# k and v made token-major by VectorE block transposes and a trip through DRAM, in place of TensorE transposes, in a one-core hybrid trunk layer

## The chip, the cores and the metric

The kernel runs on one core of a Trainium2 chip. The metric is the device time of one execution in microseconds (us), as the median of several runs. In the profile the engines are PE (TensorE matmul), PEld (TensorE weight load), DVE (VectorE), ACT (ScalarE), POOL (GpSimd) and SP (SyncE, whose one queue issues every DMA of this kernel).

## The reference

One layer over 16 meta tokens and 2048 tokens of width 1024, all in float32. The part that the change touches is the gated DeltaNet group (8 heads of 128), chunk by chunk:

```python
q, k, v = jnp.split(jax.nn.silu(causal_dwconv(qkv, dn_conv_w)), 3, axis=-1)   # then per head, q and k normalised
kk = jnp.einsum('bhnid,bhnjd->bhnij', k, k)
a_low = jnp.where(strict, beta[..., :, None] * kk * decay, 0.0)
tmat = a_low + jnp.eye(CHUNK, dtype=a_low.dtype)
u = lax.linalg.triangular_solve(tmat, v * beta[..., None], left_side=True, lower=True, unit_diagonal=True)
w = lax.linalg.triangular_solve(tmat, k * (beta * jnp.exp(g))[..., None], left_side=True, lower=True, unit_diagonal=True)
...
def step(S, inp):
    u_c, w_c, qk_c, qd_c, kd_c, gl_c = inp
    v_new = u_c - jnp.einsum('bhcd,bhde->bhce', w_c, S)
    o = jnp.einsum('bhcd,bhde->bhce', qd_c, S) + jnp.einsum('bhij,bhje->bhie', qk_c, v_new)
    S = S * gl_c[..., None, None] + jnp.einsum('bhcd,bhce->bhde', kd_c, v_new)
    return S, o
```

Beside it stand a combined input projection (1024 to 8208 columns), a short gated convolution over another 1024 channels, the output projection (2048 to 1024), the residual and a final RMSNorm.

## The kernel before

The tokens are done in two halves (`hf` 0 and 1) of 1024, the first with the 16 meta tokens. **The main stream** is a list of jobs, 64 for each half: a job is one 128-column block of the input projection. It loads its weights (`load_w`, tile `wr`, two buffers), splits them in a high and a low part (`split_w`: `wh` on ACT, `wl` on DVE) and runs 24 matmuls for each token group (`run_group`, tile `mm`). So float32 accuracy is made of three passes: `hh`x`wh`, `hl`x`wh`, `hh`x`wl`. A job's result goes through a convolution on DVE (`acc`) to `k`, `q` or `vT`, or to a gate. These tiles are channel-major: channel on the partition, token along the row. After the jobs the output projection runs in units of 48 matmuls (`unit_mm`).

**The side streams** do the DeltaNet heads, one at a time: 16 pairs of half and head, `i` = 0 to 15. `delta_front` makes the 128x128 products of k and q for the 8 chunks of a head, sends the diagonal 32x32 blocks through DRAM (`nbd`, tile `nb`), inverts them row by row on DVE (`substitution`: `prod`, `XT`) and writes the result to DRAM (`xtd`). `delta_back` reads it back to `W`, and merges the 32-blocks to 64-blocks with small matmuls (the merges: `X`, `Q`, `p1` to `p4`). It also makes the token-major operands: `kd` from `k`, `vr` from `vT`, each in two groups of four 128x128 transposes on TensorE into PSUM (pool `pta`, tag `ta`, two buffers), evicted with a scale `cd` by ACT and a scale `ir` by DVE. `delta_scan` runs the 8 chunks of the recurrence (PE `rec` and `o`, DVE `yy` and `S`, ACT `vn`), and reads `kd` and `vr`. `delta_out` normalises and gates. In the first half `normalize` also prepares rows of the second half's tokens, in the tile `kd`.

**What sets the order.** On PE, DVE, ACT and POOL the instructions run in the order in which they are written. A planner in the program sets that order: it keeps a clock of its own for each engine, and after every few matmuls of the main stream `pump()` lets each side stream that its clock calls ready write its next piece. The order of the DMAs on SP is set by the framework's scheduler. A DMA there also waits on one of eight semaphores, which it takes over from the DMA eight issues ahead. `hold(tag)` keeps two streams from one tile. Every instruction is recorded through one helper, so the profile puts nearly all of them on line L118, and tiles tell them apart.

Of the kernel before, what the change touches and what calls it, by code (L numbers as in the profile page):

```python
# [19 lines left out]
NM = 16  # L20
# [153 lines left out]
def hybrid_trunk(  # L174
# [24 lines left out]
    ged = tc.dram_tile([2, NH * 9, 128], F32, name="ged")  # L199
    nmd = tc.dram_tile([2, NM, NM], F32, name="nmd")  # L200
# [317 lines left out]
    def normalize(i):  # L518

        xt = vt(dp, [128, NC, 128], "kd").rearrange("p c i -> p (c i)")  # L520
        nc.sync.dma_start(xt, xs[HALF + 128 * i :][:128])
        yield after(xt)
        st = statistics(xt, 128, vt(dp, [128, 1840], "gw", dt=BF16))
        gains = []
        yield from hold("Q", True)

        def gain(c2):
            gains.append(vt(dp, [128, NC, 64], "Q").rearrange("p c i -> p (c i)"))
            nc.sync.dma_start(gains[c2], norm_g[0, 512 * c2 : 512 * c2 + 512].partition_broadcast(128))

        gain(0)
        yield after(gains[0], st[1])
        rs = refine(st, 128)
        for c2 in range(2):
            xc = xt[:, 512 * c2 : 512 * c2 + 512]
            nc.vector.scalar_tensor_tensor(xc, xc, rs, gains[c2], op0=ALU.mult, op1=ALU.mult)
            if c2 == 0:
                gain(1)
                yield after(gains[1])
        held.discard("Q")  # L540
        nc.sync.dma_start(xnd[i], xt)
        done.add(("xn", i))
# [34 lines left out]

    G = {}

    def gates(hf):  # L580
# [20 lines left out]
        pt = ptile(pta, "ta", [128, 512])  # L601
        gw = vt(dp, [128, 920], "gw")
# [82 lines left out]
        nc.sync.dma_start(ged[hf, :Wd], gT[:Wd])  # L685
        G[hf] = dict(beta=beta, gcum=gcum, neg=neg, nch=nch)
# [422 lines left out]

    def delta_back():  # L1110

        for i in range(2 * NH):
# [19 lines left out]
            while ("conv", hf, 16 + hd, LAST[hf]) not in done:  # L1132
                yield 0.3
            for b4 in range(2):
                cs = slice(4 * b4, 4 * b4 + 4)
                yield after(slot=(pta, "ta"), least=0.3)
                yield from hold()
                pk = ptile(pta, "ta", [128, 4, 128])
                for c in range(4):
                    tr(pk[:, c, :], k_[:, 4 * b4 + c, :])  # L1140
                for c in range(4):
                    cc = 4 * b4 + c
                    nc.scalar.activation(kd[:, cc], pk[:, c, :], AF.Copy, scale=cd[:, cc : cc + 1])
                yield after(d["vT"], slot=(pta, "ta"), least=0.3)
                yield from hold()
                pv = ptile(pta, "ta", [128, 4, 128])
                for c in range(4):
                    c0 = m0 + 128 * (4 * b4 + c)
                    tr(pv[:, c, :], d["vT"][:, c0 : c0 + 128])
                nc.vector.tensor_tensor(  # L1150
                    out=vr[:, cs],
                    in0=pv,
                    in1=ir[:, cs].unsqueeze(2).to_broadcast([128, 4, 128]),
                    op=ALU.mult,
                )
# [8 lines left out]
            done.add(("vr", i))  # L1164
# [18 lines left out]
            for a in (0, 64):  # L1183
                nc.scalar.activation(Q[a + 32 : a + 64, :, 0:32], p1[a + 32 : a + 64, :, 0:32], AF.Copy)
            nc.vector.tensor_copy(egl, qd[:, :, 127])
# [24 lines left out]
            for c in range(NC):  # L1210
                mmf(p4[0:64, c, :], lhsT=Q[64:128, c, :], rhs=W[64:128, c, 64:128])
            held.discard("Q")
            done.add(("merged", i))
            nc.scalar.mul(W[0:64, :, 64:128], p4[0:64], -1.0)
            yield after(W, qd)
# [164 lines left out]

    STEP = 1.0
# [110 lines left out]
    start(delta_front())  # L1492
    start(delta_back())
# [143 lines left out]
```

## Time and profile before

| | before |
|---|---|
| time, median of 3 runs (lowest to highest) | 2236.77 us (2235.26 to 2238.23) |
| the profiled execution's own time | 2236.26 us |
| its span from first to last instruction | 2234.5 us |
| busy share: PE, DVE, ACT, POOL | 97%, 65%, 38%, 8% |
| DMA: share of 16 engines, MB moved | 46.0%, 197.14 MB |
| mean granted TensorE clock | 0.992 of full speed |

The profiled execution stands 0.5 us under the median. Of its time 1.8 us lie outside the span. Matmuls are pipelined, so the durations of matmuls overlap, and their cost is read from the distance between starts.

### The profile page before, as it was taken

To read this page: it belongs to the slowest core of one execution; us is meant where nothing else is said; L and a number is where in the kernel's file an instruction comes from. 1 tells how busy PE (TensorE), PEld (TensorE's weight loads), DVE (VectorE), ACT (ScalarE), POOL (GpSimd) and SP (SyncE) were. 2 spreads that over 40 slices of the span, in tenths; PEclk is the share of its full clock that TensorE was granted. 3 is DMA by queue.
4 is the path that set the end of the run, shared out by engine and by line. 5 is a ranking of instruction groups with operands and counts; after the bars stand their busy time and mean duration, and the time that the engine had idled before them with its cause. 6 is when DMAs were issued, how large, how long until landed. Compare 5 with 4: busy or idle time off the path is not lost.

```text
span 2234.5 us, 35464 instructions
## 1 busy us (share of the span) xinstructions
PE 2174.5 (97%) x13472; PEld 1917.1 (86%) x13472; DVE 1451.7 (65%) x3919; ACT 854.0 (38%) x1987; POOL 189.3 (8%) x345
## 2 busy tenths in 40 slices
PE   6999999999998999999999999999999999999998
PEld 6999999999998999977888888888888877888886
DVE  4677777677775668686767677676767674444422
ACT  5533434343443334444344352425252523332211
POOL 4010101010101010111010101010101000000000
PEclk9999999999999999999999999999999999999999
DMA  5434544353446744523444423343677343645521
GB/s 140 76 77 67 86 70 95 64 95 65 92 61 78 83 76 89 131 43 60 82 70 65 83 57 78 53 78 53 79 52 75 60 114 126 203 170 188 188 91 57
DMA packets 258537, 199.41 MB, mean 89 GB/s; under 512 B 62117, under 2 KB 226478, under 8 KB 258366
## 3 DMA queue, kind: packets, MB, share of 16 engines
q1 hardware_dynamic: 258366, 197.14, 46.0%
q8 instruction: 106, 1.74, 0.3%
q14 instruction: 65, 0.53, 0.1%
HBM read 160.51 MB, written 36.59 MB: 88 GB/s over the span
## 4 chain that ended last, share of the span: by engine, by line
PE 88%; DMA 4%; DVE 3%; ACT 2%; SPq 1%; issue 1%; POOL 0%; POOLq 0%; ACTq 0%; DVEq 0%
PE mm L118 75%; PE ta L118 7%; PE rec L118 4%; PE o L118 2%; DMA kd<-in_x_dram 2%; SPq L118 1%; ACT junk L118 1%; DMA wr<-in_w_in_dram 1%; DMA nb<-nbd 1%; DVE prod L118 1%; DMA xtd<-XT 0%; DVE wl L118 0%; DVE XT L118 0%; ACT wh L118 0%; DVE acc L118 0%
## 5 line engine op out<-in xcount | busy, mean ns | idle before, releaser
L118 PE MATMUL mm<-hh,wh 128*128 128x512 f32 (+3 forms) x2816 | 1008.4, 366 | 8.7 <-ACT hh L118 6.7
L118 PE MATMUL mm<-hl,wh 128*128 128x512 f32 (+3 forms) x2816 | 985.4, 357 | 0.4 <-DVE hl L118 0.4
L118 PE MATMUL mm<-hh,wl 128*128 128x512 f32 (+3 forms) x2816 | 640.1, 360 | 1.7 <-DVE wl L118 1.7
L118 PEld LDWEIGHTS mm<-hh,wh 128*128 128x128 f32 x2816 | 533.1, 190 | 60.3 <-ACT hh L118 7.9
L118 PEld LDWEIGHTS mm<-hl,wh 128*128 128x128 f32 x2816 | 532.5, 190 | 48.1 <-DVE hl L118 1.9
L118 PEld LDWEIGHTS mm<-hh,wl 128*128 128x128 f32 x2816 | 479.6, 189 | 48.9 <-DVE wl L118 2.2
L118 DVE TENSOR_TENSOR wl<-wr,wh 128x512 fp32r<-128x512 f32 x356 | 238.3, 689 | 97.6 <-ACT wh L118 77.0
L118 DVE SCALAR_TENSOR_TENSOR acc<-raw,pcol,acc 128x384 f32<-128x384 f32 (+2 forms) x360 | 232.9, 649 | 87.9 <-ACT acc L118 83.8
L118 ACT ACTIVATE wh<-wr 128x1024 fp32r<-128x1024 f32 x182 | 191.9, 1055 | 88.7 <-PE mm L118 49.7
L118 DVE SCALAR_TENSOR_TENSOR prod<-nb,XT 128x8 f32<-128x8 f32 (+30 forms) x496 | 191.0, 385 | 22.7 <-DMA nb<-nbd 19.1
L118 DVE TENSOR_REDUCE XT<-prod 128x8 f32<-128x16 f32 (+30 forms) x496 | 147.2, 297 | 17.0
L118 ACT ACTIVATE vn<-rec,cj 128x128 f32<-128x128 f32 x128 | 46.9, 366 | 248.4 <-PE rec L118 248.1
L118 ACT ACTIVATE raw<-mm 128x384 f32<-128x384 f32 (+2 forms) x120 | 61.5, 513 | 192.7 <-PE mm L118 192.2
L118 PE MATMUL mm<-oh,wh 128*128 128x512 f32 x256 | 101.9, 398 | 0.0
L118 ACT ACTIVATE sc_c<-mm 128x384 f32<-128x384 f32 (+3 forms) x82 | 42.1, 515 | 154.4 <-PE mm L118 154.3
L118 PE MATMUL mm<-ol,wh 128*128 128x512 f32 x256 | 100.4, 392 | 0.0
L118 DVE SCALAR_TENSOR_TENSOR yy<-rec,neg,vr 128x128 f32<-128x128 f32 x128 | 44.5, 348 | 56.1 <-PE rec L118 55.5
L118 DVE TENSOR_TENSOR y<-mm,y 128x512 f32<-128x512 f32 x21 | 14.5, 691 | 101.1 <-PE mm L118 101.1
L118 ACT ACTIVATE ojk<-y 128x512 bf16<-128x512 f32 x21 | 13.2, 631 | 164.6 <-DVE y L118 127.1
L118 DVE SCALAR_TENSOR_TENSOR S<-S,egl,rec 128x128 f32<-128x128 f32 x104 | 35.7, 343 | 59.6 <-PE rec L118 59.1
L118 POOL TENSOR_TENSOR opy<-mo,nhalf 128x4 f32<-128x4 f32 x32 | 34.3, 1073 | 460.3 <-DVE mo L118 451.5
L118 POOL TENSOR_SCALAR_AFFINE_SELECT E<-E 128x1024 f32<-128x1024 f32 x16 | 18.3, 1143 | 641.8 <-PE ta L118 352.3
(240 smaller groups left out, 2574.4 us busy)
## 6 DMA issues: line engine op xcount, KB each, us to landing
wr<-in_w_in_dram SPq DMA_DIRECT2D x128, 512.0 KB, 7.8
wr<-mixd SPq DMA_DIRECT2D x54, 512.0 KB, 4.3
E<-gtd SPq DMA_DIRECT2D x16, 512.0 KB, 3.8
qd<-ged SPq DMA_DIRECT2D x16, 512.0 KB, 6.4
nb<-nbd SPq DMA_DIRECT2D x64, 128.0 KB, 2.8
mixd<-zs SPq DMA_DIRECT2D x32, 256.0 KB, 2.4
out_dram<-y SPq DMA_DIRECT2D x16, 512.0 KB, 2.7
kd<-in_x_dram SPq DMA_DIRECT2D x9, 512.0 KB, 7.6
```

What stands on the lines that cost most here:

```text
L118: r = real(*args, **kw)
```

## The change

For each head a new side stream, `delta_turn`, takes `k` as soon as its convolution is done, and `vT` as soon as its own is, in two halves of four chunks each. `turn_out` transposes the 32x32 blocks of a 128x512 half on DVE into a temporary tile (the tags `gw` and `Q`, which exist already), and four DMAs write it to a new DRAM buffer `kvd`, so that the blocks land in transposed places: each moves 32 partitions in pieces of 32 floats (128 bytes). `delta_back` then reads `kd` and `vr` back from `kvd` by one DMA each, in pieces of 128 floats. The scale `cd` is now multiplied into the whole `kd` by POOL, and `ir` into the whole `vr` by DVE. The 16 TensorE transposes of k and v and their 10 evictions per head are gone; the 8 transposes of q stay. The job of the next `vT` now waits for the copy of `vT` to be issued, not for `delta_back`.

```diff
+    kvd = tc.dram_tile([2, 2, NC, 128, 128], F32, name="kvd")
...
+    def turn_out(dram, src, tmp):
+        nc.vector.transpose(out=tmp.rearrange("p c i -> p (c i)"), in_=src.rearrange("p c i -> p (c i)"))
+        for a in range(4):
+            nc.sync.dma_start(
+                dram[:, :, 32 * a : 32 * a + 32].rearrange("c (b y) x -> y (c b) x", b=4),
+                tmp[32 * a : 32 * a + 32].rearrange("y c (b x) -> y (c b) x", b=4),
+            )
...
+    def delta_turn():
+        for i in range(2 * NH):
+            hf, hd = divmod(i, NH)
+            m0 = NM if hf == 0 else 0
+            while i >= 2 and ("blocks", i - 2) not in done:
+                yield 0.3
+            for w in range(2):
+                while ("conv", hf, (8, 16)[w] + hd, LAST[hf]) not in done:
+                    yield 0.3
+                src = slot[i]["k"] if w == 0 else slot[i]["vT"][:, m0 : m0 + HALF].rearrange("p (c i) -> p c i", i=128)
+                for c2, tag in enumerate(("gw", "Q")):
+                    yield after(src, slot=(dp, tag), eng="DVE", lag=0.3)
+                    yield from hold(tag, True)
+                    cs = slice(4 * c2, 4 * c2 + 4)
+                    turn_out(kvd[i % 2, w, cs], src[:, cs], vt(dp, [128, 4, 128], tag))
+                    if w and c2:
+                        done.add(("vr", i))
+                    yield DRAIN
+                    held.discard(tag)
+            done.add(("turned", i))
...
-            while ("conv", hf, 16 + hd, LAST[hf]) not in done:
+            while ("turned", i) not in done:
                 yield 0.3
+            for w, t_ in enumerate((kd, vr)):
+                nc.sync.dma_start(t_, kvd[i % 2, w].rearrange("c t j -> t c j"))
             for b4 in range(2):
-                cs = slice(4 * b4, 4 * b4 + 4)
-                yield after(slot=(pta, "ta"), least=0.3)
-                yield from hold()
-                pk = ptile(pta, "ta", [128, 4, 128])
-                for c in range(4):
-                    tr(pk[:, c, :], k_[:, 4 * b4 + c, :])
-                for c in range(4):
-                    cc = 4 * b4 + c
-                    nc.scalar.activation(kd[:, cc], pk[:, c, :], AF.Copy, scale=cd[:, cc : cc + 1])
-                yield after(d["vT"], slot=(pta, "ta"), least=0.3)
-                yield from hold()
-                pv = ptile(pta, "ta", [128, 4, 128])
-                for c in range(4):
-                    c0 = m0 + 128 * (4 * b4 + c)
-                    tr(pv[:, c, :], d["vT"][:, c0 : c0 + 128])
-                nc.vector.tensor_tensor(
-                    out=vr[:, cs],
-                    in0=pv,
-                    in1=ir[:, cs].unsqueeze(2).to_broadcast([128, 4, 128]),
-                    op=ALU.mult,
-                )
...
+            nc.gpsimd.tensor_tensor(
+                out=kd, in0=kd, in1=cd.unsqueeze(2).to_broadcast([128, NC, 128]), op=ALU.mult
+            )
             nc.vector.tensor_copy(egl, qd[:, :, 127])
...
+            nc.vector.tensor_tensor(
+                out=vr, in0=vr, in1=ir.unsqueeze(2).to_broadcast([128, NC, 128]), op=ALU.mult
+            )
             held.discard("Q")
             done.add(("merged", i))
             nc.scalar.mul(W[0:64, :, 64:128], p4[0:64], -1.0)
-            yield after(W, qd)
+            yield after(W, qd, kd, vr)
...
+    start(delta_turn())
     start(delta_back())
```

**PE, pair i = 11 (second half, head 3), just ahead of its merges.** `x4` counts equal instructions in a row, and `ta<-ident,k` is a transpose of k. Before:

```order
L118 MATMUL ta<-ident,k 128x128 x4
L118 MATMUL mm<-hl,wh 128x512
L118 MATMUL mm<-hh,wh 128x512
L118 MATMUL ta<-ident,vT 128x128 x4
L118 MATMUL mm<-hl,wh 128x512
L118 MATMUL mm<-hh,wl 128x512 x2
L118 MATMUL ta<-ident,q 128x128 x4
L118 MATMUL mm<-hh,wl 128x512 x6
```

After:

```order
L118 MATMUL mm<-hh,wl 128x512 x3
L118 MATMUL ta<-ident,q 128x128 x4
L118 MATMUL mm<-hh,wl 128x512 x2
L118 MATMUL ta<-ident,q 128x128 x4
L118 MATMUL mm<-hh,wl 128x512 x3
```

The groups of k and v are gone from among the matmuls of the main stream, and nothing takes their place on PE.

**SP, pair i = 12 (second half, head 4), around the read of `W`.** `xtd<-XT` writes the inverted blocks and `W<-xtd` reads them back. Before:

```order
L118 DMA wr<-in_w_in_dram 128x8x128 x3
L118 DMA xtd<-XT 32x8x32 x4
L118 DMA W<-xtd 32x8x32 x4
L118 DMA E<-gtd 128x1024
```

After:

```order
L118 DMA kd<-kvd 128x8x128
L118 DMA mixd<-sc_y 128x4x128
L118 DMA qd<-ged 128x1024
L118 DMA mixd<-sc_y 128x4x128
L118 DMA wr<-in_w_in_dram 128x8x128
L118 DMA mixd<-zs 128x4x128
L118 DMA wr<-in_w_in_dram 128x8x128
L118 DMA kvd<-gw 32x16x32 x4
L118 DMA kvd<-Q 32x16x32 x4
L118 DMA wr<-in_w_in_dram 128x8x128
L118 DMA xtd<-XT 32x8x32 x4
L118 DMA vr<-kvd 128x8x128
```

The next row is again `W<-xtd`. Eight writes of v and the read of `vr` now stand just ahead of it, and the read of `kd` some way earlier. Such a read stands between `xtd<-XT` and `W<-xtd` in 3 of the 16 pairs (5, 12 and 13).

**POOL, pair i = 11, around its new multiplication.** `E<-E` belongs to the front of the next head, and `kpy` too. After:

```order
L118 COPY raw<-qcar 128x3 x2
L118 AFFINE_SELECT E<-E 128x1024
L118 TENSOR_TENSOR kd<-kd,cd 128x1024
L118 COPY sc_u<-ucar 128x2
L118 TENSOR_TENSOR kpy<-ssk,nhalf 128x8
```

Before, `COPY sc_u` followed `AFFINE_SELECT E<-E` directly.

## Rows read from the trace of the kernel before

**Rows 1.** The page, part 1: busy us, share of the span and instructions.

```profile
PE 2174.5 (97%) x13472; PEld 1917.1 (86%) x13472; DVE 1451.7 (65%) x3919; ACT 854.0 (38%) x1987; POOL 189.3 (8%) x345
```

**Rows 2.** Stretches of 50 us: busy us (instructions), clock, DMA share, GB/s.

```profile
700.00:750.00 50.00, 46.21 (x278) 45.90 (x277) 30.31 (x114) 17.96 (x44) 3.12 (x7) 0.94 0.72 90
...
1500.00:1550.00 50.00, 50.00 (x332) 40.52 (x331) 36.43 (x69) 26.24 (x57) 1.81 (x3) 1.00 0.36 52
...
1850.00:1900.00 50.00, 46.16 (x300) 36.30 (x299) 21.15 (x41) 17.50 (x37) 1.01 (x1) 0.90 0.33 108
```

**Rows 3.** PE in order of time, pair 11: start us, us, what.

```profile
1412.32 0.60 PE L118 MATMUL ta<-ident,k 128*128 128x128 f32 x4
1412.67 0.48 PE L118 MATMUL mm<-hh,wh 128*128 128x512 f32 x1
1412.99 0.39 PE L118 MATMUL mm<-hl,wh 128*128 128x512 f32 x1
1413.22 0.60 PE L118 MATMUL ta<-ident,vT 128*128 128x128 f32 x4
```

**Rows 4.** Groups by shape, of what goes: busy us, mean ns | idle before.

```profile
L118 ACT ACTIVATE kd<-ta,cd 128x128 f32<-128x128 f32 x128 | 36.3, 369 | 17.2 <-PE ta L118 15.8 <-DMA W<-xtd 1.4
...
L118 DVE TENSOR_TENSOR vr<-ta,ir 128x512 f32<-128x512 f32 x32 | 21.9, 685 | 6.8 <-PE ta L118 6.6
...
L118 PE MATMUL ta<-ident,vT 128*128 128x128 f32 x128 | 20.5, 283 | 1.2 <-ACT junk L118 0.7
...
L118 PE MATMUL ta<-ident,k 128*128 128x128 f32 x128 | 19.7, 277 | 1.3 <-ACT junk L118 1.3
```

**Rows 5.** What PE waited for: us, times, longest.

```profile
PE ta L118 <- DVE vr L118: 2.3, 1, 2.3
```

**Rows 6.** Groups by shape nearest to the new VectorE work.

```profile
L118 DVE TENSOR_TENSOR wl<-wr,wh 128x512 fp32r<-128x512 f32 x356 | 238.3, 689 | 97.6 <-ACT wh L118 77.0 <-PE mm L118 20.2
...
L118 DVE STREAM_TRANSPOSE X<-W 32x256 f32<-32x256 f32 x48 | 20.7, 432 | 2.2 <-DMA W<-xtd 1.1
...
L118 DVE TENSOR_TENSOR E<-E,cj 128x1024 f32<-128x1024 f32 x16 | 19.9, 1245 | 0.0
```

**Rows 7.** The tile kd: ns min/median/max, first and last start us.

```profile
L118 ACT ACTIVATE kd<-ta,cd x128: 342/368/395, 198.7 to 1846.0; 128x128 f32<-128x128 f32 x128
```

**Rows 8.** All engines, from 949 us: a POOL operation beside VectorE.

```profile
949.20 0.14 DVE L118 SCALAR_TENSOR_TENSOR msm<-mnb,mXT 16x4 f32<-16x4 f32 x1
...
949.59 2.70 POOL L118 TENSOR_TENSOR wl<-wr,wh 128x1024 fp32r<-128x1024 f32 x1 [16.39 <-ACT wh L118]
...
950.27 2.04 DVE L118 SCALAR_TENSOR_TENSOR msm<-mnb,mXT 16x5 f32<-16x5 f32 x1
```

**Rows 9.** The DMA queue, then issues: KB each, median us to landing.

```profile
q1 hardware_dynamic: 258366, 197.14, 46.0%
...
wr<-in_w_in_dram SPq DMA_DIRECT2D x128, 512.0 KB, 7.8
wr<-mixd SPq DMA_DIRECT2D x54, 512.0 KB, 4.3
...
nbd<-E SPq DMA_DIRECT2D x64, 32.0 KB, 1.9
xtd<-XT SPq DMA_DIRECT2D x64, 32.0 KB, 4.2
W<-xtd SPq DMA_DIRECT2D x64, 32.0 KB, 1.9
```

**Rows 10.** SP in order of time: the reads of W of pair 11.

```profile
1418.38 1.78 SPq L118 DMA_DIRECT2D W<-xtd  x4
```

**Rows 11.** VectorE in order of time: the transposes of W, pair 11.

```profile
1424.46 0.75 DVE L118 SCALAR_TENSOR_TENSOR acc<-raw,pcol,acc 128x512 f32<-128x512 f32 x1 [6.46 <-ACT acc L118]
1425.12 1.36 DVE L118 STREAM_TRANSPOSE X<-W 32x256 f32<-32x256 f32 x3
```

**Rows 12.** The same of pair 13.

```profile
1641.41 0.43 DVE L118 STREAM_TRANSPOSE X<-W 32x256 f32<-32x256 f32 x1 [0.64 <-DMA W<-xtd]
```

More of the change, by code (lines that the diff above doesn't have):

```diff
@@ L522, in normalize @@
         yield after(xt)
+        yield from hold("gw")
         st = statistics(xt, 128, vt(dp, [128, 1840], "gw", dt=BF16))
@@ L601, in gates @@
         pt = ptile(pta, "ta", [128, 512])
+        yield from hold("gw", True)
         gw = vt(dp, [128, 920], "gw")
@@ L685, in gates @@
         nc.sync.dma_start(ged[hf, :Wd], gT[:Wd])
+        held.discard("gw")
         G[hf] = dict(beta=beta, gcum=gcum, neg=neg, nch=nch)
@@ L1163, in delta_back @@
                     nc.scalar.activation(junk[:, 0:128], pq[:, c, :], AF.Square, accum_out=ssq[:, cc : cc + 1])
-            done.add(("vr", i))
             egl = vt(dp, [128, NC], "egl")
@@ L1379, in delta_out @@
             yield 0.3
+    DRAIN = 4.0
     STEP = 1.0
```

## The prediction, made before the changed kernel was run

> **What bounds the kernel now.** First the page's busy shares [rows 1]: PE is busy 97% of the span, DVE 65%, ACT 38%, POOL 8%. A busy PE need not be a full one, so the stretches come next [rows 2]. From 1500 to 1550 us PE has no idle time at the full granted clock while DVE is busy 36.4 of 50 us: here PE runs through its written order and nothing else limits it. At 700 to 750 and at 1850 to 1900 us PE stands idle for 3.8 us each and the granted clock drops to 0.94 and 0.90; in the first of these the DMA share is 0.72, twice the 0.36 of the clean stretch. So for most of the span the time is the sum of what PE is given, and in a few stretches it is a wait in the side streams. A change that takes work off PE should therefore show nearly in full, as long as it opens no new wait there. PE takes its order as written, so any wait of a side stream that the planner's clocks did not foresee stops the main stream too.
>
> **The change part by part.**
>
> *Transposes off PE.* How much a group of four costs is read from starts, not durations, which overlap. The k group starts at 1412.32 us, the v group at 1413.22, and between them stand the k group and two matmuls [rows 3]. The second of these takes 0.23 us to the next start, so the group takes 0.90 - 2 x 0.23 = 0.44 us. There are 128 + 128 such transposes [rows 4], 64 groups: 64 x 0.44 = 28.2 us off PE. The order shows that the matmuls around them simply close up. In the clean stretches this is on the path.
>
> *Waits that stood at them.* PE waited once for the eviction of `vr`, 2.3 us [rows 5]; that goes. The idle time just before the k and v groups is 1.3 + 1.2 us in all [rows 4], put down mostly to ACT's evictions of q, which stay. I take 2.3 us, with 0 and 4.8 us as bounds.
>
> *Evictions off ACT and DVE.* 128 ACT copies of 369 ns and 32 DVE multiplications of 685 ns go [rows 4]. ACT is at 38% and off the path: I cost that at nothing.
>
> *Work onto DVE.* 64 block transposes of 128x512. The nearest rows are the same operation at 32x256, 432 ns, and another operation at 128x512, 689 ns [rows 6]. The bounds are the second and twice the first, 0.69 to 0.86 us; I take 0.70, 64 x 0.70 = 44.8 us. The 16 multiplications of `vr` at 128x1024 cost 1.245 us each as the like one [rows 6], 19.9 us, against 21.9 us that go. DVE gains 43 us, and goes from 65% to about 67%. The 13.6 us that it has free in a clean stretch of 50 [rows 2] hide this, at 2.7 us per head. A head comes round every (1846.0 - 198.7) / 15 = 110 us, by the first and the last eviction of k [rows 7]. Without that cover it would cost up to 43 us.
>
> *Work onto POOL.* 16 multiplications of `kd` at 128x1024. POOL's own multiplication of that size took 2.70 us [rows 8], so about 43 us on an engine at 8%. Its price lies elsewhere. While it ran, a tiny DVE operation with two SBUF inputs (`msm`) that had taken 0.14 us took 2.04 us [rows 8]: DVE lost 1.9 us. Everything behind it on DVE waits too: `acc`, `wl`, the scan's `yy`, and PE for those. The bounds are 0 and 16 x 1.9 = 30.4 us. POOL's new operation stands behind the select of the next head's `E`, about where DVE in pair 11 sat idle for 6.46 us just before the transposes of `W` [rows 11]. So I take a sixth, 0.3 us per head, 5 us.
>
> The Trainium skill (SBUF — State Buffer, SBUF: two separate sides) calls this an exclusive lock, held for the whole instruction, by whichever of a GpSimd operation and a DVE operation with two SBUF inputs starts first. The trace agrees so far: 2.04 us for 0.14. By the page DVE would lose up to the whole 2.70 us each time, and the sum at its worst would be 43.2 instead of 30.4 us.
>
> *DMA.* Per head 16 writes of 64 KB in 128-byte pieces and two reads of 512 KB in 512-byte pieces: 8192 + 2048 packets and 2.1 MB. Before, the queue moved 197.14 MB in 258366 packets at 46.0% of the engines' span [rows 9], 1028 us of all sixteen. By bytes a head's share is 2.1/197.14 x 1028 = 11 us, by packets 10240/258366 x 1028 = 41 us, of 110 us per head. The nearest row, `nbd<-E`, 32 KB in 256 such pieces, lands in 1.9 us [rows 9], which lies near the lower end. I take 13 us: the share goes from 46% to near 58%. A weight load lands in 7.8 us [rows 9] and is issued about a job and a half ahead, so it has room. What has little room is the read of `W`, which PE's merges wait for. In pair 11 its four issues end at 1420.2 us [rows 10]; 1.9 us of landing [rows 9] counted from the last, which is issued some 0.45 us earlier, gives 1421.6, and DVE takes `W` up at 1425.1 [rows 11]: 3.5 us of room. Pair 13 has none: DVE there waits for the DMA itself [rows 12]. Queued on SP behind the new writes, which wait for DVE's transposes, are weight loads, `xtd` and `W`; `kd` and `vr` themselves are needed only by the scan, behind the merges. I add 4 us, one more stall like that of 700 to 750 us [rows 2], for the stretches in which the queue is already full. The bounds are 0 and rival C's.
>
> The Trainium skill (DMA: Bandwidth & Descriptors, Specifications) says that pieces under 512 bytes fall short of line rate, since the engine reads, modifies and writes. No row here sets such pieces beside long ones at equal load; if the rule bites, the share goes towards the 41 us end, and the wait is that of rival C.
>
> *Sum.* Against the profiled execution's own 2236.3 us, 0.5 us under the median: 2236.3 - 28.2 - 2.3 + 5 + 4 = 2214.8, so 2215 us.
>
> **The rivals.**
>
> *A. Nothing is given back.* DVE's free time hides both the transposes and POOL's hold, and `W` lands in its room everywhere. For it: the clean stretches, and that PE hardly ever waits for DVE there [rows 2]. Against it: the full queue at 700 us. 2236.3 - 28.2 - 2.3 = 2205.8 us.
>
> *B. POOL's hold on DVE reaches PE in full.* For it: the 1.9 us that DVE lost [rows 8], which the planner's clocks do not know of. Against it: the idle DVE at that place [rows 11]. 2205.8 + 30.4 = 2236.2 us: no change. The page on SBUF would make it 2205.8 + 43.2 = 2249 us, if every hold lasted the whole operation and reached PE.
>
> *C. `W` comes late, and it ends slower.* One queue serves all. The two reads of 1 MB per head and the writes of v get between `xtd<-XT` and the landing of `W`, the merges of each head wait, and PE with them. In the order such a read stands exactly there in 3 pairs, and writes of v just ahead of it in most. Each 512 KB in 512-byte pieces lands in 4.3 to 7.8 us [rows 9], so 2.4 to 5.9 us over a small one. If `W` is late by d, a head loses d - 3.5 us: 2205.8 + 5 + 16 x (d - 3.5). It decides from d = 5.1 us on, where the gain is gone. One slow read ahead of it, d = 5.9, gives 2249 us. Against it: `xtd` itself takes 4.2 us to land [rows 9], and `W` waits for that anyway, so a read issued between the two runs beside that wait.
>
> **How the numbers follow.** My forecast, 2205 to 2226 us around 2215, gets 0.60, A 0.13, B 0.12, C 0.15. What a measurement of this kernel can tell from no change is about 0.2%, 4.5 us, so faster is under 2232.3 and slower over 2241.2. Faster: the forecast, A, and a little of B, 0.74. Same: most of B and the mild end of C, 0.12. Slower: the rest of C, 0.14. The range starts at the lower bound, 2236.3 - 28.2 - 4.8 = 2203, and reaches to 2241 over B and the mild end of C, which leaves out about 0.14.
>
> **What would show it.** Right: 256 fewer PE transposes and no `kd<-ta` on ACT; in a clean stretch PE again without idle time; about 28 us fewer between the first and last matmul there; DVE near 67% busy; block transposes near 0.70 us; `kvd` writes landing in about 2 to 4 us. The hold shows as a DVE operation with two SBUF inputs that lasts 2 us beside POOL's `kd`, with or without a PE wait on DVE behind it. Rival C shows as DVE waiting for `W<-xtd` ahead of `X` in many pairs, and PE `ta` waiting on `X`. I would be wrong if PE's idle time grows by more than about 15 us, at whatever place, or if the block transposes take well over 0.86 us, so that DVE runs behind everywhere.

## The result and the profile after

The changed kernel takes 2265.95 us (median of 4 runs, 2261.55 to 2272.59), the kernel before 2236.33 us beside it: ratio 1.0134, 95% interval 1.0107 to 1.0161. It is 30 us slower (1.3%), where 22 us faster was forecast. The profiled execution is the longest of the four, 2272.59 us with a span of 2271.0 us; the mean granted clock is 0.978, before 0.992.

The page's busy shares of the changed kernel, to be held against [rows 1]:

```profile
PE 2168.2 (95%) x13216; PEld 1911.9 (84%) x13216; DVE 1485.6 (65%) x3963; ACT 818.5 (36%) x1857; POOL 220.1 (10%) x361
```

The 256 transposes are gone from PE, yet its busy time fell by 6.3 us only, and its idle time grew from 60.0 to 102.8 us (span less busy time). The prediction had named more than 15 us of added idle time as a sign of being wrong. Stretches of the changed kernel: length, busy us of PE, PEld, DVE, ACT and POOL, then clock, DMA share and GB/s. The first three answer to [rows 2].

```profile
700.00:750.00 50.00, 47.03 (x284) 46.51 (x283) 31.13 (x113) 17.11 (x43) 2.81 (x5) 0.93 0.88 93
...
1500.00:1550.00 50.00, 50.00 (x234) 41.17 (x233) 39.31 (x97) 16.98 (x39) 2.73 (x4) 1.00 0.68 110
...
1850.00:1900.00 50.00, 41.36 (x174) 32.23 (x173) 38.65 (x89) 18.78 (x42) 3.16 (x2) 0.92 0.52 161
```

```profile
1100.00:1600.00 500.00, 495.72 (x2905) 411.28 (x2904) 372.14 (x928) 190.46 (x428) 50.54 (x67) 1.00 0.54 88
550.00:1000.00 450.00, 418.59 (x2907) 402.47 (x2906) 314.32 (x961) 165.96 (x417) 53.02 (x81) 0.95 0.64 98
1600.00:1950.00 350.00, 324.32 (x1792) 265.13 (x1791) 220.93 (x533) 121.53 (x271) 25.13 (x32) 0.95 0.65 99
```

The same three wide stretches of the kernel before:

```profile
1100.00:1600.00 500.00, 499.81 (x2975) 415.06 (x2975) 356.79 (x903) 199.02 (x470) 41.27 (x63) 1.00 0.41 68
550.00:1000.00 450.00, 432.62 (x3020) 409.93 (x3019) 320.97 (x987) 180.66 (x454) 44.62 (x78) 0.98 0.52 81
1600.00:1950.00 350.00, 341.92 (x1925) 280.13 (x1924) 221.20 (x517) 135.80 (x311) 20.25 (x27) 0.98 0.56 101
```

The middle stretch is nearly as clean as it was: PE idles 4.3 us in it, before 0.2. Most of the loss lies in the other two, where the second half's rows are prepared and where the jobs end; they are called the full stretches below. There PE idles 14.0 + 17.6 = 31.6 us more, and the clock of what it does run is lower: 418.59 x 0.05 + 324.32 x 0.05 = 37.1 us below full speed against (432.62 + 341.92) x 0.02 = 15.5, so some 22 us more. That is an estimate from clocks rounded to 0.01, but it agrees with the 28.2 us that the prediction counted off PE, of which its busy time shows 6.3. By this estimate an idle us cost nearly two here.

What PE waits for in the changed kernel (us in total, times, longest):

```profile
PE ta L118 <- DVE X L118: 21.3, 10, 9.6
PE mm L118 <- ACT hh L118: 13.2, 3, 7.1
PE ta L118 <- issue: 10.6, 4, 7.5
PE mm L118 <- DVE sc_y L118: 6.9, 1, 6.9
```

The wait on `vr` [rows 5] is gone; waits on `X`, the transposed `W`, lead instead. The DMA queue and its issues (KB each, median us to landing), beside [rows 9]:

```profile
q1 hardware_dynamic: 426094, 229.14, 55.5%
...
wr<-in_w_in_dram SPq DMA_DIRECT2D x128, 512.0 KB, 9.0
...
kvd<-gw SPq DMA_DIRECT2D x128, 64.0 KB, 5.3
kvd<-Q SPq DMA_DIRECT2D x128, 64.0 KB, 2.5
...
vr<-kvd SPq DMA_DIRECT2D x16, 512.0 KB, 7.7
kd<-kvd SPq DMA_DIRECT2D x16, 512.0 KB, 4.2
...
xtd<-XT SPq DMA_DIRECT2D x64, 32.0 KB, 4.8
W<-xtd SPq DMA_DIRECT2D x64, 32.0 KB, 2.0
```

How `W` comes late is seen in pair 13, first on SP, then on DVE:

```profile
1636.62 8.49 SPq L118 DMA_DIRECT2D kvd<-gw  x4
1645.21 4.16 SPq L118 DMA_DIRECT2D kvd<-Q  x4
1649.48 0.44 SPq L118 DMA_DIRECT2D wr<-in_w_in_dram  x1
1650.02 5.67 SPq L118 DMA_DIRECT2D xtd<-XT  x4
1655.80 0.39 SPq L118 DMA_DIRECT2D vr<-kvd  x1
1665.79 1.78 SPq L118 DMA_DIRECT2D W<-xtd  x4
```

```profile
1647.41 0.42 DVE L118 TENSOR_REDUCE XT<-prod 128x8 f32<-128x256 f32 x1
...
1667.48 0.43 DVE L118 STREAM_TRANSPOSE X<-W 32x256 f32<-32x256 f32 x1 [6.08 <-DMA W<-xtd]
```

`XT` is complete at 1647.8 us, but SP stands at eight writes until 1649.4. Its writes of `xtd` take 5.7 us to issue, with the read of `vr` behind them, and `W` is asked for at 1665.8. [Rows 12] showed 0.64 us of waiting here; now it is 6.08. The longest piece of the way is the landing of `xtd`, as the chain of work that ended last shows for this pair and for pair 14 (start us, us, what):

```profile
1655.24 10.42 DMA xtd<-XT
...
1666.63 1.81 DMA W<-xtd
...
1779.40 6.25 DMA xtd<-XT
...
1785.79 6.98 DMA W<-xtd
```

In the kernel before, pair 13 took 13.0 us from the first issue of `xtd` (1626.67 us) to that of `W` (1639.66); now it takes 15.8, and 2.2 pass before that first issue.

`W` is not the only late transfer. In the first full stretch the same chain, from 715 to 815 us, spends more on the loads of the norm's scale (`in_norm_g`) for the second half's rows. They go into the tile `Q`, which `turn_out` now uses too:

```profile
720.96 14.76 DMA Q<-in_norm_g_dram
...
764.14 18.30 DMA Q<-in_norm_g_dram
...
794.36 9.53 DMA xtd<-XT
```

DVE waits 21.8 us for these loads in the changed kernel, 0.4 in the kernel before, 13.6 in the run "no trip" below, 23.3 with thin transfers, and 1.6 with the change in ten pairs. No run takes this wait out alone.

### The profile page after: what moved, and what is told of

It reads as the page before. It is cut to its first block, busy times and chain, and to the rows that moved or that the text cites. A ratio compares the mean times of both kernels' runs of the same rounds, so it can differ in the third digit from the quotient of the medians.

```text
span 2271.0 us, 35343 instructions
## 1 busy us (share of the span) xinstructions
PE 2168.2 (95%) x13216; PEld 1911.9 (84%) x13216; DVE 1485.6 (65%) x3963; ACT 818.5 (36%) x1857; POOL 220.1 (10%) x361
## 2 busy tenths in 40 slices
DMA packets 426265, 231.39 MB, mean 102 GB/s; under 512 B 197717, under 2 KB 394846, under 8 KB 426094
## 3 DMA queue, kind: packets, MB, share of 16 engines
q1 hardware_dynamic: 426094, 229.14, 55.5%
## 4 chain that ended last, share of the span: by engine, by line
PE 79%; DMA 9%; DVE 6%; SPq 2%; ACT 2%; issue 1%; POOL 0%; POOLq 0%; DVEq 0%; ACTq 0%
PE mm L118 67%; PE ta L118 6%; PE rec L118 4%; PE o L118 2%; DMA xtd<-XT 2%; SPq L118 2%; DMA W<-xtd 2%; DMA Q<-in_norm_g_dram 1%; DMA wr<-in_w_in_dram 1%; DVE prod L118 1%; DVE acc L118 1%; DMA nb<-nbd 1%; DVE XT L118 1%; DVE wl L118 1%; ACT wh L118 0%
## 5 line engine op out<-in xcount | busy, mean ns | idle before, releaser
L118 PEld LDWEIGHTS mm<-hh,wh 128*128 128x128 f32 x2816 | 539.0, 192 | 80.3 <-ACT hh L118 14.5
L118 PEld LDWEIGHTS mm<-hl,wh 128*128 128x128 f32 x2816 | 538.8, 192 | 48.9 <-DVE hl L118 1.9
L118 ACT ACTIVATE sc_c<-mm 128x384 f32<-128x384 f32 (+3 forms) x82 | 42.2, 515 | 126.2 <-PE mm L118 125.8
L118 POOL TENSOR_TENSOR kpy<-ssk,nhalf 128x8 f32<-128x8 f32 x16 | 27.4, 1713 | 509.7 <-DVE ssk L118 482.6
```

Of the source, the lines that this page charges most:

```text
L118: r = real(*args, **kw)
```

## The experiments

All times are medians; the kernel before took 2235.8 to 2236.9 us beside them. The ratio is to that, with its 95% interval. "New order" is the order that the planner writes for the changed kernel. In it the model's `planned()` counts a transfer that is not issued, so PE, DVE, ACT and POOL keep their order; SP's order shifts a little (between thin and full writes some 20 of 711 other transfers stand elsewhere). The trip is the way of k and v through DRAM. The expectations set several theories against each other: T, the added packets fill the queue; O, SP stands in its order at the new transfers and issues the others late; D, the work added to DVE makes PE wait; P, the order that the planner newly writes is the cause.

| run | us | ratio (interval) |
|---|---|---|
| new order: no trip, no block transposes | 2219.2 | 0.9919 (0.9903 to 0.9936) |
| no trip | 2228.8 | 0.9970 (0.9957 to 0.9983) |
| reads alone | 2227.9 | 0.9962 (0.9947 to 0.9977) |
| 4 thin writes per head, thin reads | 2245.5 | 1.0034 (1.0022 to 1.0045) |
| 16 thin writes per head, thin reads | 2251.5 | 1.0066 (1.0049 to 1.0083) |
| full writes, no reads | 2267.7 | 1.0137 (1.0107 to 1.0167) |
| whole change, writes on POOL's queue | 2262.5 | 1.0124 (1.0098 to 1.0149) |
| own orders: writes 1 us later, on ACT's queue | 2330.4 | 1.0420 (1.0400 to 1.0440) |
| writes 1 us later, on SP's queue | 2291.2 | 1.0240 (1.0207 to 1.0273) |
| before without k's and v's transposes, planned anew | 2247.9 | 1.0050 (1.0035 to 1.0066) |
| old order: the same, planned as before | 2229.3 | 0.9966 (0.9954 to 0.9979) |
| plus block transposes | 2240.7 | 1.0014 (1.0002 to 1.0026) |
| plus writes | 2309.7 | 1.0333 (1.0313 to 1.0353) |
| whole change | 2283.3 | 1.0213 (1.0187 to 1.0238) |
| change in ten pairs (0 to 3, 7 to 12) | 2229.1 | 0.9969 (0.9958 to 0.9979) |
| change in six pairs (4 to 6, 13 to 15) | 2285.4 | 1.0219 (1.0201 to 1.0236) |
| change in eight pairs (2, 3, 7 to 12) | 2238.6 | 1.0005 (0.9993 to 1.0016) |
| ten pairs, writes on POOL's queue | 2254.3 | 1.0075 (1.0061 to 1.0089) |

### What part of the trip costs

**No trip.** The transfers go, and POOL and DVE multiply straight from `k` and `vT`.

```diff
-            nc.sync.dma_start(
+            planned(
                 dram[:, :, 32 * a : 32 * a + 32].rearrange("c (b y) x -> y (c b) x", b=4),
...
-                nc.sync.dma_start(t_, kvd[i % 2, w].rearrange("c t j -> t c j"))
+                planned(t_, kvd[i % 2, w].rearrange("c t j -> t c j"))
...
-                out=kd, in0=kd, in1=cd.unsqueeze(2).to_broadcast([128, NC, 128]), op=ALU.mult
+                out=kd, in0=k_, in1=cd.unsqueeze(2).to_broadcast([128, NC, 128]), op=ALU.mult
```

> The changed kernel with the same order of instructions on PE, DVE, ACT and POOL, but without the 18 DMAs per head: kd is multiplied straight from k and vr from vT, so that they hold the wrong layout. Theory T, that the added packets fill the one DMA queue and that small transfers which PE waits for come late: the loss goes, 2200 to 2215 us. Theory O, that SP stands in its order at the new writes and their semaphores and so issues the other transfers late: the same, 2200 to 2215 us. Theory D, that the work added to DVE and POOL makes PE wait: 2250 to 2270 us as in the changed kernel.

**Thin transfers.** As no trip, with all 18 transfers issued at their places, but 32 short pieces each.

```diff
+            tc.nc.sync.dma_start(dram[0, 0:32, 32 * a : 32 * a + 32], tmp[32 * a : 32 * a + 32, 0, 0:32])
...
+                tc.nc.sync.dma_start(t_[0:32, 0, :], kvd[i % 2, w, 0, 0:32])
```

> As the one without the trip, but all 18 DMAs per head are issued, in their places and with their waits, each moving 32 pieces instead of 512 (the writes) or 1024 (the reads). The data moved is left out for the rest. Theory T: nearly as fast as without the trip, 2205 to 2220 us, since the packets are gone. Theory O: as slow as the changed kernel, 2245 to 2270 us, since SP's issues and waits are all there. Theory D: 2250 to 2270 us.

**Writes alone** (the reads become `planned`), and **reads alone** (from the input, whose place is known early; no writes):

```diff
+                tc.nc.sync.dma_start(
+                    t_, xs[1024 * w : 1024 * w + 1024, 128 * hd : 128 * hd + 128].rearrange("(c t) j -> t c j", t=128)
+                )
```

> The changed kernel with its 16 writes per head in full, 8192 pieces of 128 bytes, but without the two reads back: kd and vr are made from k and vT in the wrong layout. Theory T with the time by packets: most of the loss stays, 2245 to 2265 us. Theory T with the time by bytes: about half of it, 2225 to 2245 us. Theory O: most of it, 2245 to 2265 us, since 16 of 18 issues are there.

> The changed kernel with its two reads per head of 512 KB in 512-byte pieces, taken from the input x instead of the copy of k and v, and without the 16 writes; kd and vr hold other data. Theory T by packets: little loss is left, 2205 to 2225 us. Theory T by bytes: about half, 2220 to 2245 us. Theory O: little, 2205 to 2220 us.

The reads cost nothing: 2227.9 against 2228.8 us without them, and leaving them out of the whole change gives nothing back. The writes cost 38.9 us (2267.7 - 2228.8): 22.7 by thin transfers being issued at all (the two thin reads among them) and 16.2 more by full packets. By the intervals of the runs the first is good to about 5 us and the second to about 8, so T and O both hold, and which is the larger is not settled. Matmul set against matmul, the kernel with writes is 4.7 us ahead of the one without at 550 us, 20.0 late at 1000, 15.6 at 1600 and 41.8 at 1950. The lateness of `W` alone goes more with the packets: from the last `XT` to the last landing of `W` that is recorded, summed over the 16 pairs, it takes 162 us in the kernel before, 182 without the trip, 191 with thin transfers and 229 in the changed kernel. And without any trip some 20 us are missing against 2236.5 - 28.2, which the next run takes up.

**No block transposes either**, the DVE time counted in the plan only:

```diff
-        nc.vector.transpose(out=tmp.rearrange("p c i -> p (c i)"), in_=src.rearrange("p c i -> p (c i)"))
+        to, ti = tmp.rearrange("p c i -> p (c i)"), src.rearrange("p c i -> p (c i)")
+        model.issue("DVE", nc.vector.cost("transpose", [to], [ti], (), {}), [to], [ti])
```

> As the kernel without the trip (2228.8 us), with the same order on every engine, but the 64 block transposes on VectorE are left out too; the scales are multiplied straight into untransposed k and v, so the output is not the layer's. The kernel without the trip stands some 20 us above 2208 us, which is the kernel before less 28.2 us of TensorE transposes. Theory D (VectorE's added work makes TensorE wait): most of those 20 us go, 2208 to 2216 us. Rival P (it is the order which the planner now writes, with the holds on `gw` and `Q`, whatever VectorE does): 2224 to 2229 us.

2219.2 us: 9.6 us of the 20 are the block transposes (D in part). The rest stays.

**Four thin writes per head** instead of 16:

```diff
+            if a == 3:
+                tc.nc.sync.dma_start(dram[0, 0:32, 0:32], tmp[0:32, 0, 0:32])
```

> As the kernel with thin transfers (2251.5 us; it stands 22.7 us over the kernel without the trip), with the order of PE, VectorE, ACT and POOL kept, but one thin write in place of four for each half: 4 writes per head instead of 16. k and v are scaled untransposed, so the output is not the layer's. If it is the number of transfers on SP, with a semaphore for each: a quarter of the cost is left, 2234 to 2240 us. If it is SP's wait for the block transposes, which each half still has: 2247 to 2253 us.

It fell between the two expectations: of the 22.7 us, 6.0 go with three quarters of the writes. Most of it is there with one waiting transfer per half and two thin reads; the count of transfers matters less.

### Another queue

**Writes from ACT's queue, and the same late issue from SP's**: `turn_out` keeps the transpose, and the four DMAs follow when the plan has it done.

```diff
+                    yield after(tmp, least=1.0)
+                    send_out(kvd[i % 2, w, cs], tmp)
                     yield DRAIN
```

> The whole change, with the 16 writes per head issued from ACT's queue instead of SP's, about 1 us after their block transpose, so that neither ACT nor SP waits for VectorE at them. Theory O (SP stands at the writes, and the other transfers go out late): the 22.7 us that the issues alone cost go, 2240 to 2247 us; what is left over the kernel without the trip is the packets'. Theory T (the packets fill the DMA engines, whoever issues them): 2260 to 2270 us.

> The same kernel with the same late issue of the writes, but from SP's queue: beside it the kernel with ACT's queue differs in the queue alone. Theory O, if it is the wait for the block transposes at which SP stands: 2245 to 2252 us, as with ACT's queue. If it is the order on SP and its eight semaphores, or the packets (T): 2260 to 2270 us.

Both are far off every expectation. The later issue also makes the planner write another order, so SP's 2291.2 us says nothing clean of the wait. Beside it ACT's queue is 39 us slower still: ACT itself waits there for the DMAs (31.8 us for `kvd<-Q` ahead of `ucar`), and PE waits 31.6 us for `os` and 17.3 for ACT's `vn`.

**Writes from POOL's queue**, nothing moved on PE, DVE and ACT:

```diff
-            nc.sync.dma_start(
+            tc.nc.gpsimd.dma_start(
                 dram[:, :, 32 * a : 32 * a + 32].rearrange("c (b y) x -> y (c b) x", b=4),
```

> The whole change with the right output and the order of PE, VectorE and ACT kept; the writes of k and v are issued from POOL's queue instead of SP's, with the same packets. Theory O (SP's order and semaphores): the 22.7 us of the issues go and the 15 us of the packets stay, about 2243 us. Theory T (packets alone): 2260 to 2270 us. Rival Q: POOL itself is held at its issues, and the waits on POOL's results (the selects and powers) make it slower than 2270 us.

2262.5 us, its interval overlapping that of the whole change, so Theory O's 2243 us did not come, nor Rival Q's over 2270. What PE waits for there, and the two queues (packets, MB, share):

```profile
PE rec L118 <- DVE os L118: 13.6, 5, 7.5
PE ta L118 <- issue: 12.8, 6, 7.3
PE mm L118 <- ACT hh L118: 11.8, 3, 5.7
...
PE ta L118 <- DVE X L118: 2.6, 5, 0.8
```

```profile
q1 hardware_dynamic: 290926, 212.35, 49.9%
q0 software_dynamic: 8192, 16.79, 3.4%
```

PE's wait on `X` fell from 21.3 to 2.6 us, and other waits took its place. But the run doesn't tell what the late `W` is worth. DVE still waits for `W<-xtd` ahead of `X`, 18.6 us in seven waits (38.4 in ten in the changed kernel). And POOL pays for the move: its writes wait 352.2 us for DVE's `gw`, and DVE waits 10.6 us for POOL's `prod` ahead of `XT`, before the move 0.3. Matmul set against matmul, this kernel takes 9.3 us less than the changed one from 550 to 1000 us and 14.3 less from 1600 to 1950 (part of this can be that the changed kernel's profile is its slowest execution), and loses 10.3 us from 450 to 500 and 6.6 from 1550 to 1600. So a gain on SP and a loss on POOL can be mixed in this one time.

### Was the gain there at all

**Before without the 256 transposes**, planned anew:

```diff
-                pk = ptile(pta, "ta", [128, 4, 128])
                 for c in range(4):
-                    tr(pk[:, c, :], k_[:, 4 * b4 + c, :])
+                    model.issue("PE", nc.tensor.cost("transpose", [k_[:, 0, :]], [k_[:, 0, :]], (), {}), [], [k_])
...
-                    nc.scalar.activation(kd[:, cc], pk[:, c, :], AF.Copy, scale=cd[:, cc : cc + 1])
+                    nc.scalar.activation(kd[:, cc], k_[:, cc, :], AF.Copy, scale=cd[:, cc : cc + 1])
```

> The kernel before, in which only the 256 TensorE transposes of k and v are left out; ACT and VectorE then scale k and v untransposed from SBUF in the same places, so the output is not the layer's. The planner still counts the transposes. If the 28.2 us of the prediction is right: 2206 to 2209 us. If the transposes lay partly beside waits that stay: 2215 us or more.

11 us slower than before, though PE has 256 instructions fewer and DVE, ACT and POOL have none more. **The same in the old order**: a stand-in for the PSUM tile keeps the planner's clocks as they were.

```diff
-                pk = ptile(pta, "ta", [128, 4, 128])
+                pk = model.tile(pta, "ta", 2, Stand(_Tensor(f"pk{i}_{b4}"), 512))
                 for c in range(4):
-                    tr(pk[:, c, :], k_[:, 4 * b4 + c, :])
+                    model.issue("PE", 0.109, [pk], [k_])
```

> The kernel before with the 256 TensorE transposes of k and v left out, as in the run that came out 11 us slower than before, but now the plan is kept: the planner counts every left-out instruction and its PSUM tile, so TensorE, VectorE, ACT and POOL have the order of before with nothing changed but the missing transposes (SP's differs by two transfers that change places). ACT and VectorE scale k and v untransposed, so the output is not the layer's. Theory P (the gain is there, and it was the newly written order that lost it): 2206 to 2212 us. Rival N (the transposes stood beside waits and are worth little wherever they are taken out): 2225 us or more.

The time is where Rival N had it: 6.6 us gained of 28.2. N's reason is another matter. With one order on PE the two traces can be set against each other matmul by matmul: across a group that is left out, the lead grows by 0.45 us in the median of the 64 groups, so at their places the transposes were worth what the prediction counted (0.44). Net of waits it is less. The first `rec<-yy,W` of head 8 and of head 12 on PE, in the kernel before:

```profile
1142.25 0.38 PE L118 MATMUL rec<-yy,W 128*128 128x128 f32 x2
...
1544.18 0.38 PE L118 MATMUL rec<-yy,W 128*128 128x128 f32 x2
```

and in the one without transposes:

```profile
1138.22 0.38 PE L118 MATMUL rec<-yy,W 128*128 128x128 f32 x2
...
1534.99 0.38 PE L118 MATMUL rec<-yy,W 128*128 128x128 f32 x2
```

It is 4.03 us ahead at the first and 9.19 at the second: 5.16 us over four heads, 1.29 us per head or 0.32 per group, since even here PE idles 2.0 us from 1100 to 1600 us (before 0.2). Over 16 heads that would be 20.6 us. But elsewhere leads shrink: one of 3.85 us at 660 us is 2.10 at 794, and one of 8.00 at 1765 is 3.29 at 1877. Over the whole span PE's busy time falls by 17.0 us only (2174.5 to 2157.5), at a mean granted clock of 0.986 against 0.992, and its idle time grows from 60.0 to 73.8. So the lead is lost about half to waits and half to the clock; that the waits are for side work which doesn't start earlier because PE has less to do is a reading, not shown.

**The old order, built up**: block transposes, then the writes, then (separately) the whole change, all unseen by the planner.

```diff
+                    tc.nc.vector.transpose(
+                        out=tmp.rearrange("p c i -> p (c i)"), in_=src[:, cs].rearrange("p c i -> p (c i)")
+                    )
...
+                        tc.nc.sync.dma_start(
+                            kvd[i % 2, w, cs, :, 32 * a : 32 * a + 32].rearrange("c (b y) x -> y (c b) x", b=4),
```

> The kernel before in its own order without the TensorE transposes, plus the 64 block transposes on VectorE, which the planner does not see, and no trip through DRAM. The output is not the layer's. Taking these transposes out of the kernel without the trip gave 9.6 us. Theory D: 5 to 10 us over the kernel in the old order without them. If VectorE's free time hides them, as the prediction had it: under 3 us.

> The same, plus the 16 writes per head to DRAM, which nobody reads. The output is not the layer's. In the new order the writes cost 39 us. Theory T or O (it is the writes themselves, by their packets or by SP standing at them): again 30 to 40 us over the kernel with the block transposes alone. Theory P (the new order has no room for a late transfer, the old one has): under 20 us.

> The whole change with the right output, but the planner does not see it: it counts the old transposes and evictions, and all engines keep the order of before, with the block transposes, the writes, the two reads and the two multiplications put between. Theory P: clearly under the changed kernel's 2266 us, 2215 to 2240 us, and it may beat the kernel before. Theory T or O: 2245 us or more, and not far from the changed kernel.

The block transposes cost 11.4 us (9.6 in the new order), the writes 69 (38.9 there). The writes fit neither expectation; that they cost more here speaks against P. The whole change in the old order takes 2283.3 us: P falls as the reason for the loss, since the planner's new order is 17 us better for the change than the old one. That the writes without a reader cost more than the whole change is not explained. Set against the kernel before, the whole change in this order comes to the first `rec<-yy,W` of a head 3.3 us early at 434 us, 7.5 late at 661, 36.8 late at 794, 43.4 at 903, still 42.2 at 1544, and 53.9 at 1653. Nothing is lost between 903 and 1544.

### Which heads

```diff
+    TRIP = (0, 1, 2, 3, 7, 8, 9, 10, 11, 12)
...
-        for i in range(2 * NH):
+        for i in TRIP:
...
+                if not trip:
+                    yield after(slot=(pta, "ta"), least=0.3)
...
+                        tr(pk[:, c, :], k_[:, 4 * b4 + c, :])
```

> The change for the ten pairs 0 to 3 and 7 to 12 alone; the other six keep TensorE's transposes. Right output. Between 1000 and 1600 us a head without the transposes gained 1.1 to 1.6 us in the old order, and the losses arose in pairs 4 to 6 and 13 to 15. If the stretch decides: 10 x 1.35 = 13.5 us less than before and little back, 2220 to 2232 us, faster than both kernels. If the trip costs alike in all heads: 30 x 10 / 16 = 19 us more than before, 2250 to 2260 us.

> The other half of that split: the change for the six pairs 4 to 6 and 13 to 15 alone. Right output. If the stretch decides: nearly the whole loss with little of the gain, 2262 to 2285 us. If the trip costs alike in all heads: 30 x 6 / 16 = 11 us more than before, 2245 to 2250 us.

The wide stretches with the change in ten pairs, then in the other six:

```profile
550.00:1000.00 450.00, 429.48 (x3012) 407.25 (x3012) 323.57 (x988) 179.50 (x453) 47.45 (x78) 0.98 0.57 86
1100.00:1600.00 500.00, 497.52 (x2923) 412.52 (x2923) 368.70 (x931) 190.12 (x433) 51.78 (x68) 1.00 0.54 87
1600.00:1950.00 350.00, 340.31 (x1919) 278.80 (x1918) 219.38 (x512) 136.51 (x312) 19.19 (x27) 0.99 0.55 102
```

```profile
550.00:1000.00 450.00, 412.28 (x2890) 395.75 (x2889) 307.99 (x954) 167.38 (x420) 51.29 (x80) 0.96 0.61 94
1100.00:1600.00 500.00, 497.33 (x2952) 411.21 (x2950) 357.19 (x900) 200.20 (x466) 38.54 (x55) 1.00 0.42 68
1600.00:1950.00 350.00, 328.26 (x1801) 268.21 (x1800) 223.81 (x535) 121.08 (x270) 26.37 (x37) 0.95 0.62 99
```

Ten pairs at 0.997, six at 1.022: 56 us between them, and the idle time and the low clock stand where the six are. The stretch decides, as far as two orders can show it: the two halves do not add up, -7 and +49 us against +30 for all sixteen, so six pairs alone cost more than the whole change. The ten pairs beat the kernel before by 0.3%, clear of the noise, and the changed one by 1.6%. Two attempts at more failed: pairs 0 and 1 taken out too (`TRIP = (2, 3, 7, 8, 9, 10, 11, 12)`), and the ten pairs with POOL's queue (the edit of above).

> The change for the eight pairs 2, 3 and 7 to 12. Right output. If pairs 0 and 1 cost more than their 2.7 us of gain (TensorE ran up to 9 us late at 250 to 350 us): 2222 to 2227 us. If they do not: 2229 to 2234 us, 1.35 us per head more than with ten.

> The change for the ten pairs 0 to 3 and 7 to 12 (2229.1 us), with their writes issued from POOL's queue and the order of PE, VectorE and ACT kept. Right output. In all sixteen heads the move took TensorE's waits for `X` from 21.3 to 2.6 us, but other waits came in their place and the time fell by 3 us only. If SP's order costs in these ten heads too: 2222 to 2226 us. If not, or if POOL's own delay takes its place: 2228 to 2236 us.

Eight pairs give no change, which fits neither expectation; each choice of pairs also makes the planner write an order of its own, and that alone was worth 18.6 us above (2247.9 against 2229.3). In the run with eight pairs DVE waits 23.7 us for the loads of the norm's scale into `Q`, with ten 1.6. So the 0.3% belongs to that one order. POOL's queue costs 25 us with every other engine's order kept; there `rec<-os` (9.6 us) and `hh` (8.6 us) lead PE's waits. Why was not followed up.

## Why the prediction was wrong

- **The step that failed is the 4 us "for the stretches in which the queue is already full".** It was priced at one more stall like that of 700 to 750 us; the writes cost 38.9 us. In the profiled executions they lose 24.7 us from 550 to 1000 and 26.2 from 1600 to 1950, and gain some 9 elsewhere. The first row of [rows 2] already showed a DMA share of 0.72 and a clock of 0.94. The room of `W` was read in pair 11, a clean one, and the loads into the tile `Q`, for which DVE waits 21.8 us, were not among the transfers with little room.
- **"A change that takes work off PE should show nearly in full"** failed too. The count was right at its place, 0.45 us per group against 0.44, but of 28.2 us only 6.6 are left in the old order: 13.8 come back as idle time of PE, and about as much as a lower clock. In the new order, with the evictions and multiplications moved as well, 17.3 are left. The wait on `vr`, 2.3 us, went as forecast.
- **"The 13.6 us that it has free in a clean stretch of 50 hide this"**: the size was right, 0.700 to 0.704 us per block transpose, and DVE's 1485.6 us in all are 34 more than before (43 forecast). The cover was not whole: 9.6 and 11.4 us came through, in the old order at about 700 to 800 and from 1600 us on, in the new order more than half (6.2 us in the profiled executions) between 900 and 1450, in clean heads too. From run to run the new order goes 2219.2 + 9.6 + 22.7 + 16.2 - 1.7 for the reads = 2266.0, which closes because each step is a difference of two runs.
- **POOL's hold** was 5 us of DVE, as sized. It came in four of 16 heads; the two operations at 199 us, of which the first otherwise takes about 0.4 us (2.18 less the 1.76 that it lost):

```profile
198.98 2.18 DVE L118 TENSOR_TENSOR sc_y<-sc_y,sc_c 128x256 f32<-128x256 f32 x1 [1.39 <-ACT sc_c L118]
198.99 1.89 POOL L118 TENSOR_TENSOR kd<-kd,cd 128x1024 f32<-128x1024 f32 x1
```

  Rival B is out: the operation took 1.92 us on average, not 2.70, and mostly met no DVE operation with two SBUF inputs. The Trainium skill (SBUF — State Buffer, SBUF: two separate sides) calls the hold an exclusive lock for the whole instruction; the trace agrees, 1.76 us of 1.89.
- **DMA load**: (0.555 x 2271.0 - 0.460 x 2234.5) / 16 = 14.5 us per head against 13 taken, nearer the bound by bytes than that by packets. (The share of 58% held for the heads' time alone; over the whole span 13 us per head make 1236 of 2215 us, 55.8%, and 55.5% came.) The writes in 128-byte pieces took 0.522 x 2270.6 - 0.476 x 2228.8 = 124.4 us of the sixteen engines, and the reads, the same 16.8 MB in 512-byte pieces, 0.504 x 2225.8 - 0.476 x 2228.8 = 60.9. The Trainium skill (DMA: Bandwidth & Descriptors, Specifications) has pieces under 512 bytes fall below line rate. The trace agrees as far as it goes, 124.4 us against 60.9, but the one are writes and the other reads. The share stayed far from the 41 us end. Of the landings forecast at 2 to 4 us, 2.5 held and 5.3 did not.
- **Rival C** named the right side and the right place, DVE waiting for `W<-xtd` ahead of `X`: 38.4 us in ten waits, against 1.1 in [rows 6], and 21.3 on PE. Of its two causes the reads were wrong, which cost nothing (2227.9 us against 2228.8), and the writes right. Its price, the same for 16 heads, was wrong too: 30.3 of the 38.4 us fall on pairs 5, 6, 13 and 14. Whether it is the whole cause is not shown: the loads into `Q` are late as well, and POOL's queue brought costs of its own.

Shown is that the writes of k and v on SP's queue make the loss, and in which stretches. Open is how it divides between the late `W` and the late loads into `Q`, and how the 22.7 us split between SP's waits for DVE and what stands behind them: neither a temporary tile other than `Q` nor a cleaner order on SP alone was tried.

## What to carry to other kernels

Price a new wait in the stretch that is already late, not in the clean one: there work taken off the busiest engine bought little here (6.6 of 28.2 us), and transfers that wait for an engine held up others behind them, with the clock on top, while reads of the same bytes cost nothing. Ask of each temporary tile who else loads into it. Move work to a trip through DRAM only where the profile shows the queue with room, head by head. And where a planner writes the order, run the removal alone in the old and in a new order first, as the order's own spread (here 18.6 us) can be as large as the gain.

## What was not expected of the hardware

- From 1780 to 1820 us of the changed kernel PE was busy 30.16 of 40 us, and the granted clock was 0.74, a mean of its two levels (2.4 and 1.2 GHz). From 768 to 808 us PE was busy only 23.92 us, at 0.80. The row of the first:

```profile
1780.00:1820.00 40.00, 30.16 (x216) 24.01 (x215) 19.59 (x49) 9.79 (x21) 0.00 (x0) 0.74 0.30 52
```

- The same writes, 16.79 MB in 128-byte pieces, count as 8192 packets from POOL's queue, and q1 of SP loses 426094 - 290926 = 135168. They take 3.4% of the engines' span there (76.8 us), while SP's queue is relieved of 0.555 x 2271.0 - 0.499 x 2260.3 = 132.5 us. The time of the kernel did not follow (2262.5 us against 2266.0).
